# Hybrid SSD and latent-attention layer on one core: twenty softmax scalings from VectorE to GpSimd, with a new order of the instructions

## The chip, the cores and the metric

The kernel runs on one core of one Trainium2 chip. The metric is the device time of one execution in microseconds (us). The engines go by the profile's names: PE is TensorE, PEld its weight loads, DVE is VectorE, ACT is ScalarE, POOL is GpSimd, SP is SyncE.

## The reference, cut to what matters

One layer is computed for two groups of tokens that share the weights: 512 first-chunk tokens, and 64 tokens of a running stream with 256 cached keys. After a norm and an input projection the layer has two branches, a chunked state-space scan (SSD) and latent attention (MLA, 8 heads); both are concatenated, projected, and followed by a SwiGLU feed-forward network of width 2816 and a last norm. What the change touches is the softmax of the attention:

```python
s = (jnp.einsum('bqhl,bkl->bhqk', ql, keys_c, ...)
     + jnp.einsum('bqhr,bkr->bhqk', qr, keys_r, ...))
mask = k_chunk[None, :] <= (qp // CHUNK)[:, None]
s = jnp.where(mask, s * scale, -jnp.inf)
pr = jax.nn.softmax(s, axis=-1).astype(keys_c.dtype)
return jnp.einsum('bhqk,bkl->bqhl', pr, keys_c)
```

Ahead of it the scan's output is gated and normalised, and that result meets the attention's output in `w_out`:

```python
y = y.reshape(b, T, SSD_WIDTH) * jax.nn.silu(z.astype(jnp.float32))
y_ssd = rmsnorm(y, p['ssd_norm']).astype(x.dtype)
...
x = x + jnp.concatenate([y_ssd, o], axis=-1) @ p['w_out']
```

## The kernel before, in words

Activations lie transposed, channels on the 128 partitions and all 576 tokens (512 + 64) along the free axis. Products of full precision are made of three products of rounded halves (`hi` and `lo`, lines 127, 128 and 157, 159): ACT rounds a tile to `hi`, DVE subtracts to get `lo`. Where a weight comes in, ACT casts `wh_...` and DVE makes `wl_...`.

The stages in time: input projection and convolution (to about 87 us), SSD chunks together with the projections `z` and the values `V` (to about 142 us), attention together with the first half of the output projection (to about 214 us), the rest of the output projection, the feed-forward network (to about 590 us), last norm and output.

SSD chunk c (lines 512 to 606): `chunk_a` loads the decay sums `cumb` and makes `xdt` from `ps_x` (L530) and `bt`; `chunk_e` forms on ACT the decays `E` (eight exponentials, L551) and on DVE the end weights `xw` (L500) and the product of `E` with `ps_b` (L560); `chunk_b` multiplies them on PE into `ps_y` (L573), which DVE adds to `xsd` (L578), and adds the carried state through `ps_i` (L584 to 586); `chunk_s` carries the state `h` on (L503, L606). `gate(c)` multiplies `xsd` with the gate `sz` (L629), squares it on ACT (L631) and adds the squares on POOL (L632, L633). A gate tile `sz` is made by `z_tile`: `zh` from `ps_z` (L476), `zt` by a tanh on ACT (L479), their product `sz` on DVE (L480).

After the last gate `norm_y` (line 808) sums over channels on PE (`ps_g`, L810 and L812), forms the factor R on ACT and DVE (`nr_y`, `nr_u`; L186 to L193), spreads it by PE over all partitions (`ps_ry`, L821) and copies it to `Ry` (ACT L825, and POOL L818 for 64 columns). `cat_tile(t)` then scales the four tiles of `xsd` with `Ry` (DVE L828) and splits them into `cat_y` (ACT L157, DVE L159). These are the operands of the first half of the output projection: PE `ps_o` (L465), added to the residual by DVE (L797). Its tiles are PE's reserve of work during attention.

Attention goes by four pairs of heads p. `pair_proj(p)` makes `qs` and `ks` from `ps_q` and `ps_k` (copies L669 and L673), with the rotary rows of `qs` brought by four DMAs from POOL's queue (L663); two buffers of `qs` are used in turn, so that pair 2 waits for the scores of pair 0. `scores(p, i)` has five blocks of queries, i = 0 to 3 with 128 (i + 1) keys for both heads j = 0 and 1, and i = 4, the stream, 128 rows with 320 keys. `soft(p, i)` makes the probabilities `pr` of a block:

```python
for j, s in enumerate(scs):
    dve.tensor_reduce(mx[:, j : j + 1], s, AX, ALU.max, negate=True)
    act.activation(pr[:, j], s, AF.Exp, bias=mx[:, j : j + 1], accum_out=sm[:, j : j + 1])
dve.reciprocal(sm[:, :n], sm[:, :n])
for j in range(n):
    if j:
        act.activation(pr[:, j], pr[:, j], AF.Identity, scale=sm[:, j : j + 1])
    else:
        dve.tensor_scalar(pr[:, j], pr[:, j], sm[:, j : j + 1], None, ALU.mult)
```

These are lines 702 to 709. The last one, L709, runs once a block, 20 times in all. `turn` and `turn_s` transpose the scaled `pr` on PE (`ptp`, L741 and L749) and copy it to `pt`; `values` multiplies it with `V` (`pv`, L766 and L777), and `cat` splits the result (L758, L759).

The order of the work is written out by hand: `issue_in_order` at the end of the kernel chains all instructions of each engine in the order of a table `ISSUE`, one list of numbers an engine, and a second table `PLACES` says which buffer of a pool a tile takes. Each engine runs its list in order and waits where an operand is not there yet. The score tiles `sc` have three PSUM banks in turn, so that a score waits until the exponential of the third score before it has been taken.

Of the kernel before, what the change touches and what calls it, by code (L numbers as in the profile page):

```python
# [11 lines left out]
F32 = mybir.dt.float32  # L12
F32R = mybir.dt.float32r
AF = mybir.ActivationFunctionType
ALU = mybir.AluOpType
# [4 lines left out]
P = 128  # L20
# [36 lines left out]
def hybrid_layer_kernel(ctx: ExitStack, tc: tile.TileContext, a, o):  # L57
    nc = tc.nc
    pe, act, dve, pool, sp = nc.tensor, nc.scalar, nc.vector, nc.gpsimd, nc.sync
# [632 lines left out]
    att_, ap_ = open_pool("att", bufs=1, side="right")  # L692
    prs, pts = {}, {}

    def soft(p, i, scs, nk):

        n = len(scs)
        mx = ap_.tile([P, 2], F32, tag="mx", name="mx", bufs=4)
        sm = ap_.tile([P, 2], F32, tag="sm", name="sm", bufs=4)
        pr = ap_.tile([P, n, nk], F32, tag=f"pr{i}", name=f"pr_{p}_{i}", bufs=2)  # L700
        for j, s in enumerate(scs):
            dve.tensor_reduce(mx[:, j : j + 1], s, AX, ALU.max, negate=True)
# [3 lines that stand above are left out]
            if j:  # L706
                act.activation(pr[:, j], pr[:, j], AF.Identity, scale=sm[:, j : j + 1])
            else:
                dve.tensor_scalar(pr[:, j], pr[:, j], sm[:, j : j + 1], None, ALU.mult)  # L709
        prs[p, i] = pr  # L710
# [689 lines left out]
808-810 792 811-824 835-842 829 849 825-826 850-851 832 830 852 843 833 853 844-845 870 854 846 855-857 847-848  # L1400
858-860 834 871 861-862 872 863 886 873 864-868 887 869 890-892 888 893-895 889 878-885 874-877 896-898 902 911
903-907 912-920 899-901 925 921-924 926-927 908-910 940 949-950 928-931 934 932-933 951-952 935 941-944 953 936-937
954 938-939 955 945-948 956-963 988 964 1000 965 972 989-990 1001-1003 991 973 966 1004-1005 967 992 1006 968 993-994
976-978 995-996 1007-1009 997 979 998-999 969 1010-1011 980 970 981 971 1014-1016 1028-1030 1017 974 982 1018-1019 975
985 1034 983 1035 984 1036-1037 986 1031-1032 987 1038 1033 1039 1044-1049 1012-1013 1020-1027 1066-1071 1060
1072-1074 1061-1062 1040 1050 1075 1042 1051 1076 1041 1077 1063-1064 1043 1052 1065 1053 1078-1089 1054 1106-1107
1090 1108-1112 1056-1057 1055 1113-1117 1058 1130 1059 1091 1131-1132 1100 1118-1125 1133 1092 1126-1127 1134
1128-1129 1135-1137 1104 1101 1138 1096 1214-1217 1097 1139-1140 1098 1218 1141 1099 1219-1221 1105 1093 1222 1143
1094 1223 1142 1102 1226-1227 1224 1228-1231 1095 1225 1103 1232-1235 1144 1236-1237 1161 1145 1250-1251 1162 1146
1252-1254 1238-1241 1164-1165 1255-1257 1242-1243 1173 1166 1244 1167 1258 1245 1163 1168 1259 1246-1249 1155-1160  # L1410
1147-1154 1190-1191 1178 1262 1175-1176 1174 1177 1263 1179 1260 1169 1264 1180 1265-1266 1170 1267 1261 1171 1268
1172 1269 1212-1213 1187 1270 1181 1271 1182 1274 1183 1275 1184 1272 1185 1276 1186 1277 1188 1278 1273 1189
1279-1282 1200-1205 1192-1199 1206-1207 1303 1209 1304 1208 1305 1210 1306 1211 1283 1307 1284-1286 1308 1287-1288
1309 1289-1290 1315 1292 1316 1293 1317 1291 1310 1296 1318 1297 1311 1298-1299 1319 1294-1295 1312 1300 1313 1301
1314 1302 1320 1333-1336 1327-1332 1337-1340 1321-1326 1341-1376 1389-1391 1377-1379 1392-1396 1380 1397-1404
1381-1388 1405-1435 1437 1436 1438-1459 1572 1460 1569 1461-1470 1560 1566 1471-1484 1570 1485-1492 1563-1564 1557
1493-1496 1573 1561 1497-1514 1565 1584 1515 1585 1516-1519 1521 1520 1558 1522-1527 1567 1528 1568 1529 1559 1574
1530-1536 1571 1537-1538 1593 1590-1591 1539-1540 1562 1581 1545-1547 1582-1583 1592 1548-1550 1541-1544 1578
1551-1552 1587 1579-1580 1553-1556 1575-1576 1602 1577 1594 1588 1596 1595 1614 1599 1586 1603 1597 1589 1611 1598
1600-1601 1620 1604 1617 1612 1605-1606 1621-1622 1615 1608-1609 1607 1613 1632 1610 1643 1626-1628 1633 1616  # L1420
1635-1636 1629 1644-1649 1623 1641 1624 1630 1650 1625 1651-1654 1618-1619 1638 1637 1631 1679-1682 1655-1660 1639
1667 1661-1662 1668 1683 1663 1634 1642 1684-1685 1669-1670 1640 1671-1673 1686 1664-1665 1674 1687 1675-1676 1666
1688 1677 1689 1703-1704 1678 1690-1699 1715 1705-1706 1716 1700-1702 1707-1714 1717-1719 1727-1732 1763-1765 1733
1720-1721 1734 1739 1722 1735-1736 1766 1740 1737 1767 1741-1743 1751 1768-1773 1744-1748 1723 1738 1724 1787 1774
1752-1758 1725-1726 1749 1788 1750 1759-1760 1789-1791 1761 1792-1797 1775 1798 1776-1777 1762 1778-1786 1799
1823-1830 1847 1831 1848-1849 1832 1850-1857 1800 1811 1801 1812-1813 1833 1858 1814 1834 1802-1804 1815-1816
1835-1836 1859-1860 1817 1861-1869 1818-1819 1837-1839 1820-1821 1840-1843 1871 1844-1846 1805-1807 1870 1872 1822
1808 1873-1878 1883 1809-1810 1879 1895-1901 1880-1881 1902-1906 1884-1889 1882 1919-1920 1890-1893 1921-1922
1931-1935 1907-1909 1955 1936 1923 1956 1910 1924 1911-1915 2009 1894 1937-1938 1916-1917 1939-1940 2010-2011 1918
2012 1941 2013 1957-1958 2014 1959 1943-1945 1925-1930 1960 1946 1942 2039-2041 1947-1949 2027-2028 1997-1999  # L1430
1985-1986 1950-1953 1961 1954 2029 1987-1988 2000 2042 2001 1962-1964 1989-1990 2043 2030 1973 2031 2033-2034
1974-1975 1965 1991 2003-2004 1966 1992 2005 1976 2002 2032 1967 2006 1993-1994 2035 1977 2044 2036 1978 1968 2007
1995 2037 1996 1979-1981 2038 1982-1983 2008 2045 2051 2046-2047 2052 1969 2021 2063-2065 2048-2049 1984 2053-2055
1970 2050 1971 2015-2017 2066 2056-2058 1972 2069 2059-2061 2070 2022 2018-2019 2062 2067 2071-2073 2023 2020 2075
2068 2099 2074 2100-2101 2076-2081 2102-2107 2024-2026 2082-2083 2087 2108 2088 2177 2089-2092 2084-2086 2093-2098
2111-2113 2123 2109 2124-2126 2114-2119 2127-2128 2120 2129-2133 2121-2122 2134-2136 2178-2181 2165-2166 2110
2141-2146 2167 2182 2153-2154 2137 2155-2156 2147-2150 2138 2195 2151 2207-2208 2196-2199 2157 2200 2159 2168 2201
2158 2139-2140 2213 2160 2152 2161-2162 2214 2202 2169 2163 2215-2216 2170 2209 2164 2217 2210-2212 2218-2219 2171
2183 2172-2175 2220-2221 2184 2176 2185-2186 2237 2222-2230 2203 2187-2189 2238 2204-2205 2239 2190 2206 2255
2191-2192 2256-2260 2267 2240 2243 2241-2242 2193 2268 2231-2232 2244-2246 2233 2269 2261-2264 2194 2247-2248 2234  # L1440
2265 2249 2235-2236 2270-2274 2291 2266 2275-2278 2250-2254 2292-2305 2279-2290 2339 2351-2353 2306-2307 2315-2319
2308-2310 2327 2320-2321 2340-2341 2322-2323 2342 2328-2329 2354 2311 2343 2324 2344 2312 2325 2345-2346 2330-2334
2313 2335-2338 2347 2355-2356 2326 2357 2314 2358 2348 2363-2364 2349-2350 2359-2361 2365-2368 2387 2369 2388-2390
2370-2371 2375-2379 2372-2374 2391 2380-2386 2362 2399-2409 2392-2393 2411-2413 2394-2395 2410 2414 2396 2415 2423
2459 2424 2460 2425-2428 2416 2435-2436 2429 2397 2430 2417-2419 2398 2461 2420-2421 2437-2438 2422 2431 2462-2463
2513-2514 2432 2447-2450 2515 2451 2464 2452-2454 2433-2434 2455-2457 2439-2443 2458 2516-2518 2465-2469 2489 2444
2501 2490 2445 2543 2470-2472 2477 2491 2446 2473 2531 2478-2479 2532-2533 2480 2492 2502 2481 2493-2494 2482 2503
# [238 lines left out]
```

## Time and profile before

| what | value |
| --- | --- |
| median of three runs | 630.3 us (630.15 to 630.4) |
| the profiled execution, its own time | 630.52 us |
| its span, first to last instruction | 628.8 us |
| busy: PE / PEld | 618.6 / 591.4 us |
| busy: DVE / ACT / POOL | 553.9 / 387.0 / 83.1 us |
| mean granted clock of PE | 0.997 |
| HBM read and written | 59.14 MB, 4.15 MB |

The profile is that of one execution. Matmuls are pipelined and their ends are modelled, so a PE that counts as busy may still start fewer matmuls than it could; weight loads overlap with them. In a row of the timeline stand its start, its length, engine, line, operation, the tiles written and read, the shape, and, in brackets, the engine's idle time before it and what ended it. In a row of a group, the busy time, the mean of one in ns, and the idle time follow after the bars. Numbers of instructions stand behind an x.

### The profile page before, as it was taken

To read this page: it belongs to the slowest core of one execution; us is meant where nothing else is said; L and a number is where in the kernel's file an instruction comes from. 1 tells how busy PE (TensorE), PEld (TensorE's weight loads), DVE (VectorE), ACT (ScalarE), POOL (GpSimd) and SP (SyncE) were. 2 spreads that over 40 slices of the span, in tenths; PEclk is the share of its full clock that TensorE was granted. 3 is DMA by queue.
4 is the path that set the end of the run, shared out by engine and by line. 5 is a ranking of instruction groups with operands and counts; after the bars stand their busy time and mean duration, and the time that the engine had idled before them with its cause. 6 is when DMAs were issued, how large, how long until landed. Compare 5 with 4: busy or idle time off the path is not lost.

```text
span 628.8 us, 11891 instructions
## 1 busy us (share of the span) xinstructions
PE 618.6 (98%) x4591; PEld 591.4 (94%) x4591; DVE 553.9 (88%) x979; ACT 387.0 (62%) x744; POOL 83.1 (13%) x123
## 2 busy tenths in 40 slices
PE   9999999999999999999999999999999999999995
PEld 9899999976887899999999999999999999999994
DVE  6899996999876799999999997799888998999766
ACT  7555336689767489766556565555665656645454
POOL 1332241232100000000112001100210011100023
PEclk9999999999999999999999999999999999999998
DMA  9512195332311222322467137460764274725005
GB/s 314 211 36 95 36 222 153 101 101 104 118 68 34 102 101 78 112 82 68 117 161 191 54 120 186 105 167 11 200 173 114 68 185 112 188 70 185 22 1 185
DMA packets 32889, 74.64 MB, mean 119 GB/s; under 512 B 3882, under 2 KB 11960, under 8 KB 32576
## 3 DMA queue, kind: packets, MB, share of 16 engines
q1 hardware_dynamic: 26688, 62.73, 30.7%
q0 software_dynamic: 5424, 10.57, 9.4%
q8 instruction: 36, 0.59, 0.4%
q10 hardware_dynamic: 720, 0.57, 0.3%
q14 instruction: 21, 0.17, 0.1%
HBM read 59.14 MB, written 4.15 MB: 101 GB/s over the span
## 4 chain that ended last, share of the span: by engine, by line
PE 95%; DVE 2%; ACT 1%; issue 0%; DVEq 0%; POOL 0%; ACTq 0%; POOLq 0%
PE ps_x L947 21%; PE ps_z L947 11%; PE ps_dx L1087 9%; PE ps_o L465 8%; PE ps_in L143 8%; PE ps_y L947 5%; PE ps_dz L1087 5%; PE ps_z L465 4%; PE ps_l L1157 3%; PE ps_first L143 3%; PE ps_dy L1087 2%; PE ps_p L947 2%; PE sc L719 2%; PE pv L766 1%; PE ptp L741 1%; PE ps_q L465 1%
## 5 line engine op out<-in xcount | busy, mean ns | idle before, releaser
L947 PE MATMUL ps_x<-xop,wh_gu_S 128*128 128x288 f32 x504 | 120.8, 296 | 0.0
L947 PEld LDWEIGHTS ps_x<-xop,wh_gu_S 128*128 128x128 f32 x504 | 86.1, 188 | 0.6 <-ACT u L1016 0.3
L947 PE MATMUL ps_x<-xop,wl_gu_S 128*128 128x288 f32 x252 | 73.9, 295 | 0.0
L947 PE MATMUL ps_z<-xop,gu_a 128*128 128x288 f32 x252 | 57.5, 295 | 0.0
L127 ACT CAST wh_gu_S<-gu 128x1024 fp32r<-128x1024 f32 x44 | 46.0, 1052 | 15.8 <-PE ps_y L947 7.0
L128 DVE TENSOR_TENSOR wl_gu_S<-gu,wh_gu_S 128x1024 fp32r<-128x1024 f32 x44 | 53.4, 1223 | 1.5 <-ACT wh_gu_S L127 1.2
L1100 POOL DMA_DIRECT2D x<-db x16 | 14.6, 945 | 279.2 <-ACT db L1093 243.8
L947 PEld LDWEIGHTS ps_x<-xop,wl_gu_S 128*128 128x128 f32 x252 | 47.2, 188 | 0.0
L143 PE MATMUL ps_in<-xs,wh_in 128*128 128x288 f32 x256 | 45.4, 297 | 0.0
L947 PE MATMUL ps_z<-xop,wh_gu_S 128*128 128x288 f32 x168 | 42.6, 295 | 0.0
L947 PE MATMUL ps_y<-xop,wh_gu_A 128*128 128x288 f32 x168 | 42.2, 295 | 0.0
L947 PEld LDWEIGHTS ps_z<-xop,gu_a 128*128 128x128 f32 x252 | 41.9, 188 | 0.0
L947 PE MATMUL ps_x<-xop,wh_gu_A 128*128 128x288 f32 x168 | 40.1, 295 | 0.0
L143 PEld LDWEIGHTS ps_in<-xs,wh_in 128*128 128x128 f32 x256 | 37.7, 188 | 0.7 <-ACT wh_in L127 0.5
L127 ACT CAST wh_gu_A<-gu 128x1024 fp32r<-128x1024 f32 x22 | 23.1, 1050 | 15.4 <-PE ps_x L947 11.2
L465 PE MATMUL ps_o<-cat_y,wh_out 128*128 128x288 f32 x128 | 31.9, 329 | 0.1
L128 DVE TENSOR_TENSOR wl_gu_A<-gu,wh_gu_A 128x1024 fp32r<-128x1024 f32 x22 | 26.9, 1224 | 3.6 <-ACT wh_gu_A L127 2.5
L947 PEld LDWEIGHTS ps_y<-xop,wh_gu_A 128*128 128x128 f32 x168 | 29.3, 188 | 0.1
L947 PEld LDWEIGHTS ps_z<-xop,wh_gu_S 128*128 128x128 f32 x168 | 29.4, 188 | 0.0
L947 PEld LDWEIGHTS ps_x<-xop,wh_gu_A 128*128 128x128 f32 x168 | 28.6, 188 | 0.0
L143 PE MATMUL ps_in<-xs,wl_in 128*128 128x288 f32 x128 | 27.8, 295 | 0.0
L465 PE MATMUL ps_z<-xs,wh_z 128*128 128x288 f32 x128 | 27.5, 306 | 0.0
(611 smaller groups left out, 2017.8 us busy)
## 6 DMA issues: line engine op xcount, KB each, us to landing
gu<-in_w_gu SPq DMA_DIRECT2D x44, 512.0 KB, 4.6
db<-in_w_down SPq DMA_DIRECT2D x16, 512.0 KB, 4.6
x<-db POOLq DMA_DIRECT2D x16, 288.0 KB, 5.5
x<-dc POOLq DMA_DIRECT2D x16, 288.0 KB, 4.2
wr_in<-in_w_in SPq DMA_DIRECT2D x8, 512.0 KB, 5.0
wr_out<-in_w_out SPq DMA_DIRECT2D x8, 512.0 KB, 3.3
cumb<-cumD SPq DMA_DIRECT2D x5, 512.0 KB, 5.6
x<-in_xT SPq DMA_DIRECT2D x2, 1152.0 KB, 5.8
```

The costliest lines, as they stand in the source:

```text
L127: act.copy(hi, raw)
L128: dve.tensor_tensor(lo, raw, hi.bitcast(F32), ALU.subtract)
L143: pe.matmul(ps[:m, hf, :n], w, x[:, hf * n : (hf + 1) * n], start=start and k == 0 and i == 0, stop=stop and k == last and i == 2,)
L465: pe.matmul(ps[:, :n], w, x[:, cols], start=not onto and k == 0 and i == 0, stop=onto or (k == len(terms) - 1 and i == 2), skip_group_chec ...
L719: pe.matmul(s[:, :nk], qs[:, j, q0 : q0 + P], ks[:, j, :nk], start=True, stop=True)
L741: pe.transpose(pp[:, k : k + P], prs[p, i][:, j, b * P : b * P + P], ident)
L766: pe.matmul(pv[64 * j : 64 * j + 64, b * P :], V[b][:, h * HD : (h + 1) * HD], pts[p, b, j], start=b == 0, stop=True, skip_group_check=b > 0,)
L947: pe.matmul(ps, p, q, start=not onto and first and kp == kps[0] and j == 0, stop=onto or (last and kp == kps[-1] and j == 2), skip_group_c ...
L1087: pe.matmul(ps, l, r, start=not onto and k == 0 and j == 0, stop=onto or (k == n - 1 and j == 2), skip_group_check=onto,)
L1100: pool.dma_start(x2[t], v, accum_op=ALU.add)
L1157: pe.matmul(ps, w, x[:, cols], start=first and not onto and k == 0 and i == 0, stop=onto or (last and k == len(terms) - 1 and i == 2), ski ...
```

## The change

Three edits. L709 is issued on POOL and not on DVE. The small tiles `mx` and `sm` (two columns) have 20 buffers and not 4. The `ISSUE` lists of PE, DVE and ACT are ordered anew between the end of the SSD chunks and the beginning of the feed-forward network, and POOL's list has 20 entries more. SP's list and the table `PLACES` stay as they are.

```diff
@@ -695,8 +695,8 @@
         n = len(scs)
-        mx = ap_.tile([P, 2], F32, tag="mx", name="mx", bufs=4)
-        sm = ap_.tile([P, 2], F32, tag="sm", name="sm", bufs=4)
+        mx = ap_.tile([P, 2], F32, tag="mx", name="mx", bufs=20)
+        sm = ap_.tile([P, 2], F32, tag="sm", name="sm", bufs=20)
...
             else:
-                dve.tensor_scalar(pr[:, j], pr[:, j], sm[:, j : j + 1], None, ALU.mult)
+                pool.tensor_scalar(pr[:, j], pr[:, j], sm[:, j : j + 1], None, ALU.mult)
...
     "POOL": """
...
-58-59 70-71 68-69 72-85 87 86 88-89 91 90 92-97 99 98 100-101 103 102 104-105 107 106 108-118 120-121 119 123 122
+58-59 70-71 68-69 73 72 74-75 82-84 76 85 77-80 88-91 81 87 86 93 92 94-96 99 98 97 100-105 107 106 108-109 111 110
+112-117 119 118 120-121 123 122 124-125 127 126 128-138 140-141 139 143 142
```

Three places show what the lists do. The first is DVE's list near the end of the SSD chunks (minus: before, plus: changed); `zh_1516` is the last gate tile's projection, `sz<-zt_1398` the tile before it, `wl_pair` the weights of pair 1.

```order
 L500 TENSOR_TENSOR xw_1506<-xdt_1484,E_1496 128x512
 L560 TENSOR_TENSOR E_1496<-E_1496,ps_b_1486 128x512
+L480 SCALAR_TENSOR_TENSOR sz<-zt_1398,zh_1397 128x576
 L476 SCALAR_TENSOR_TENSOR zh_1516<-ps_z_0_1518,R_99 128x288
 L560 TENSOR_TENSOR E_1496<-E_1496,ps_b_1486 128x512
 L476 SCALAR_TENSOR_TENSOR zh_1516<-ps_z_1_1544,R_99 128x288
-L480 SCALAR_TENSOR_TENSOR sz<-zt_1398,zh_1397 128x576
+L128 TENSOR_TENSOR wl_pair_1816<-wr_pair_1813,wh_pair_1815 128x384
```

The older `sz` has moved ahead of the first half of `zh_1516`, and the weights of pair 1 have moved up.

The second place is PE's list at `ps_y` of chunk 3 (`ps_y_1836`); `ps_q` and `ps_k` here are projections of pair 0, `ps_s` and `ps_i` the states.

```order
+L507 MATMUL ps_s_1830<-xw_1707,bt_1615 128x256
+L465 MATMUL ps_k_1_1798<-ckv,wh_pair_1754 128x416 x2
+L465 MATMUL ps_q_1_1804<-cqn_487,wh_pair_1754 128x288
 L465 MATMUL ps_q_1_1804<-cqn_487,wl_pair_1755 128x288
-L507 MATMUL ps_s_1830<-xw_1707,bt_1615 128x256
+L465 MATMUL ps_k_1_1798<-ckv,wl_pair_1755 128x416
 L573 MATMUL ps_y_1836<-E_1734,xdt_1722 64x128 x8
-L465 MATMUL ps_k_1_1798<-ckv,wh_pair_1754 128x416 x2
-L465 MATMUL ps_k_1_1798<-ckv,wl_pair_1755 128x416
```

The second half of pair 0's `k` projection has moved from behind `ps_y` of chunk 3 to ahead of it.

The third place is the beginning of attention, on two engines. On DVE, from the scaling of pair 0's block 2 to the first `cat_y`:

```order
-L709 TENSOR_SCALAR pr_2_1967<-pr_2_1967,sm 128x384
+L828 SCALAR_TENSOR_TENSOR xsd<-xsd,par,Ry 128x576
+L702 TENSOR_REDUCE mx<-sc_s 128x1
 L828 SCALAR_TENSOR_TENSOR xsd<-xsd,par,Ry 128x576
 L704 RECIPROCAL sm<-sm 128x2
-L702 TENSOR_REDUCE mx<-sc_s 128x1
-L709 TENSOR_SCALAR pr_0_1981<-pr_0_1981,sm 128x128
-L828 SCALAR_TENSOR_TENSOR xsd<-xsd,par,Ry 128x576
 L702 TENSOR_REDUCE mx<-sc_3_0_1999 128x1
 L159 TENSOR_TENSOR cat_y_1936<-xsd,cat_y_1936 128x576
```

Two scalings are gone from between the `Ry` products, and the rest stands in nearly the same order. On POOL, at the same time (`qs_382` is the buffer of pairs 0 and 2):

```order
 L633 TENSOR_TENSOR R_99<-ysq_1860 128x128
+L709 TENSOR_SCALAR pr_3_1927<-pr_3_1927,sm 128x512
 L818 COPY Ry<-R_99 128x64
-L663 DMA qs_382<-rrp 16x576 x4
+L709 TENSOR_SCALAR pr_1_1953<-pr_1_1953,sm 128x256
+L709 TENSOR_SCALAR pr_2_1967<-pr_2_1967,sm 128x384
+L663 DMA qs_382<-rrp 16x576 x3
+L709 TENSOR_SCALAR pr_0_1981<-pr_0_1981,sm 128x128
+L663 DMA qs_382<-rrp 16x576
+L709 TENSOR_SCALAR pr_4_1994<-pr_4_1994,sm 128x320
```

The five scalings of pair 0 stand around the copy to `Ry` and the four DMAs that bring the rotary rows of pair 2.

More of the change, by code (lines that the diff above doesn't have):

```diff
@@ new lines @@
+819 811 810 821 825 827 835 812 836 854 829 828 830-831 839 837-838 844 841 858 845 840 855 850 847 856 851-853 846
+849 863 848 859 864 862 876 857 870 861 880 882 871-872 860 877 873 879 884 881 865 883 874 887 842 878 885 892 894
+866 895 886 896 893 867 843 888 868 891 897 890 889 898-901 910 875 904 911 905 902 906 869 903 912 907 914 908 913
+909 919 917 923 918 916 920 915 922 921 924-925 927 926 928-929 931 936 933 932 930 934-935 939 937 942 938 946 943
+940 947 941 944 949 945 950-951 948 952-958
```

322 lines of the change are left out of this document (158 added, 164 removed).

## The prediction

> **What bounds the kernel now.** I read the page first, then a table of busy time by stage, then TensorE's own waits in the stage that is left.
>
> ```profile
> span 628.8 us, 11891 instructions
> ...
> PE 618.6 (98%) x4591; PEld 591.4 (94%) x4591; DVE 553.9 (88%) x979; ACT 387.0 (62%) x744; POOL 83.1 (13%) x123
> ...
> PE 95%; DVE 2%; ACT 1%; issue 0%; DVEq 0%; POOL 0%; ACTq 0%; POOLq 0%
> ```
>
> The chain that ended last is 95% PE, so a faster VectorE is worth only what PE waits for it. The table by stage (columns: stretch, length, then busy us and instructions of PE, PEld, DVE, ACT, POOL, the granted clock, DMA) says where that is:
>
> ```profile
> 115.00:155.00 40.00, 38.69 (x264) 30.33 (x263) 38.61 (x83) 34.32 (x86) 10.95 (x17) 1.00 0.36 113
> 155.00:215.00 60.00, 60.00 (x451) 48.93 (x450) 42.76 (x106) 39.93 (x106) 1.92 (x4) 1.00 0.18 63
> 215.00:560.00 345.00, 344.96 (x2591) 343.87 (x2590) 321.20 (x518) 214.61 (x373) 27.71 (x32) 1.00 0.45 122
> ```
>
> Between 115 and 155 us VectorE is busy 38.6 of 40 us and PE falls short; from 155 to 215, where most of the twenty scalings stand, VectorE has 17 us to spare and PE none. So the change can only pay in the 40 us in which the last SSD chunks end and attention begins. There PE and its weight loads wait as follows (in brackets: idle time before the row, and what ended it):
>
> ```profile
> 135.72 0.95 PEld L573 LDWEIGHTS ps_y<-E,xdt 128*64 128x64 f32 x16 [0.91 <-ACT qs L669]
> 139.77 0.30 PEld L810 LDWEIGHTS ps_g<-R,ones 128*128 128x128 f32 x2 [0.40 <-issue]
> 141.96 0.30 PEld L465 LDWEIGHTS ps_q<-cqn,wh_pair 128*128 128x128 f32 x2 [0.81 <-ACT ks L673]
> 143.79 0.30 PEld L719 LDWEIGHTS sc<-ks,qs 100*128 100x128 f32 x2 [0.62 <-ACT pr L703]
> 147.48 0.97 PEld L821 LDWEIGHTS ps_ry<-R,ident 128*128 128x128 f32 x8 [0.42 <-DVE R L193]
> 149.68 0.30 PEld L719 LDWEIGHTS sc<-ks,qs 100*128 100x128 f32 x2 [0.68 <-ACT pr L703]
> 151.25 0.50 PEld L741 LDWEIGHTS ptp<-ident,pr 128*128 128x128 f32 x3 [0.42 <-DVE pr L709]
> 153.25 0.19 PEld L465 LDWEIGHTS ps_o<-cat_y,wh_out 128*128 128x128 f32 x1 [0.73 <-DVE cat_y L159]
> ```
>
> ```profile
> 135.75 1.16 PE L573 MATMUL ps_y<-E,xdt 128*64 128x128 f32 x16 [0.54 <-ACT ks L673]
> ...
> 143.80 0.70 PE L719 MATMUL sc<-ks,qs 100*128 100x256 f32 x2 [0.21 <-ACT pr L703]
> ...
> 147.49 1.16 PE L821 MATMUL ps_ry<-R,ident 128*128 128x128 f32 x8 [0.23 <-DVE R L193]
> ```
>
> The eight idle times of the weight loads add up to 5.0 us; part of that is covered by matmuls still running. PE's own three add up to 1.0 us; those leave out short gaps. The truth lies between, and I take the middle, 3 us, as all that can be won. The last of these waits is for VectorE's `cat_y`; behind it PE has dense work.
>
> **The change part by part.** The twenty scalings cost VectorE this:
>
> ```profile
> L709 DVE TENSOR_SCALAR pr<-pr,sm x20: 277/382/486, 145.4 to 204.6; 128x512 f32<-128x512 f32 x4, 128x256 f32<-128x256 f32 x4, 128x384 f32<-128x384 f32 x4, 128x128 f32<-128x128 f32 x4
> ```
>
> 20 x 0.38 = 7.6 us, but only those ahead of the first `cat_y` lie on the path. These are the rows of VectorE and ScalarE that make it:
>
> ```profile
> 112.84 0.67 ACT L479 ACTIVATE zt<-zh 128x576 f32<-128x576 f32 x1
> ```
> ```profile
> 117.89 0.46 DVE L476 SCALAR_TENSOR_TENSOR zh<-ps_z,R 128x288 f32<-128x288 f32 x1 [0.66 <-PE ps_z L465]
> ...
> 145.37 0.47 DVE L709 TENSOR_SCALAR pr<-pr,sm 128x512 f32<-128x512 f32 x1
> ...
> 146.61 0.35 DVE L192 TENSOR_TENSOR nr_u<-nr_u,nr_v 128x192 f32<-128x192 f32 x1
> ...
> 149.24 0.41 DVE L709 TENSOR_SCALAR pr<-pr,sm 128x384 f32<-128x384 f32 x1
> 149.73 0.82 DVE L828 SCALAR_TENSOR_TENSOR xsd<-xsd,par,Ry 128x576 f32<-128x576 f32 x1
> ...
> 150.92 0.28 DVE L709 TENSOR_SCALAR pr<-pr,sm 128x128 f32<-128x128 f32 x1
> 151.11 0.81 DVE L828 SCALAR_TENSOR_TENSOR xsd<-xsd,par,Ry 128x576 f32<-128x576 f32 x1
> ...
> 152.44 0.75 DVE L159 TENSOR_TENSOR cat_y<-xsd,cat_y 128x576 fp32r<-128x576 f32 x1
> ```
> ```profile
> 145.90 0.36 ACT L189 ACTIVATE nr_u<-nr_y 128x192 f32<-128x192 f32 x1
> ...
> 148.68 0.58 ACT L825 COPY Ry<-ps_ry 128x512 f32<-128x512 f32 x1
> ```
>
> Four terms, in order of time:
>
> 1. *The new order alone.* At 117.89 VectorE had waited 0.66 us for PE. The new order puts the gated tile `sz` (L480) there, whose `zt` was ready at 112.84 + 0.67 = 113.5. VectorE is full from there to the last SSD gate, so all behind comes 0.66 us earlier. ScalarE's exponentials of chunk 2 and 3 are moved up too and should keep pace; it is busy 34.3 of these 40 us.
> 2. *nr_u.* Its input from ScalarE is there at 145.90 + 0.36 = 146.26, it starts at 146.61: the queue ahead of it held the first scaling (0.47 us). That is gone: 0.35 us.
> 3. *The first L828.* `Ry` is there at 149.26, L828 starts at 149.73 behind the scaling of 149.24: 0.47 us.
> 4. *The second L828.* The scaling at 150.92 takes 0.19 us until L828 starts at 151.11.
>
> Sum 1.67 us, by which the first `cat_y` comes earlier. PE's reordering (a `k` projection ahead of `ps_y` of chunk 3) covers the 0.91 us wait at 135.72, but by itself only moves it: PE would meet the same chain later. It is counted at nothing; what it costs if the cover fails is that 0.91 us again. PE's later reorderings, the ScalarE order and four more changes of matmul kind are nothing as well, since the same work stands in a stage in which PE is never idle. The 20 instead of 4 buffers of `mx` and `sm` are two columns each; no row waits for them, nothing.
>
> What POOL's scaling costs is not in the trace. Nearest rows of POOL, one input, then two:
>
> ```profile
> L545 POOL TENSOR_SCALAR_AFFINE_SELECT cumb<-cumb 128x1024 f32<-128x1024 f32 x4 | 4.4, 1110 | 15.4 <-ACT el L520 15.4
> ...
> L632 POOL TENSOR_TENSOR ysq<-ysq 128x256 f32<-128x256 f32 x4 | 2.9, 732 | 12.4 <-ACT ysq L631 12.4
> ...
> L1248 POOL TENSOR_TENSOR ss<-ss,sq 128x320 f32<-128x320 f32 x3 | 2.6, 871 | 60.5 <-ACT sq L1243 60.4
> ...
> L818 POOL COPY Ry<-R 128x64 f32<-128x64 f32 x1 | 0.2, 236 | 3.0 <-DVE R L193 3.0
> ```
>
> With one input 64 columns take 236 ns and 1024 take 1110: (1110 - 236) / 960 = 0.91 ns a column, so 512, 384, 320, 256 and 128 columns take 0.64, 0.53, 0.47, 0.41 and 0.29 us, 2.34 us a pair of heads. With two inputs it is (871 - 732) / 64 = 2.17 ns a column, 1.29, 1.01, 0.87, 0.73 and 0.45 us, 4.35 us a pair. A scaling has one input of that size, so I take the first and keep the second for the range. POOL has 58 us of idle time between 155 and 215, so its total is covered.
>
> In POOL's queue stand DMAs too:
>
> ```profile
> 149.85 2.02 POOL L663 DMA_DIRECT2D qs<-rrp  x4 [2.12 <-PE sc_s L725]
> ```
>
> They wait for PE's last score of pair 0, about 0.5 us each. Three of them are now ahead of the scaling of `pr_0_0`, which the first transposes need: it would start at 149.85 + 1.5 = 151.35, less the 0.7 to 1 us by which the scores come earlier, and VectorE did it at 150.92. Nothing, give or take 0.3. Their own landing moves by up to 1.5 us; `qs` of pair 2 is read some 15 us later.
>
> Last, a price for running both engines at once. The same VectorE instruction with two SBUF inputs, `xw`, first alone, then while POOL reads SBUF:
>
> ```profile
> 115.74 0.69 DVE L500 TENSOR_TENSOR xw<-xdt,E 128x512 f32<-128x512 f32 x1
> ...
> 127.16 1.39 DVE L500 TENSOR_TENSOR xw<-xdt,E 128x512 f32<-128x512 f32 x1
> ```
> ```profile
> 126.93 1.08 POOL L545 TENSOR_SCALAR_AFFINE_SELECT cumb<-cumb 128x1024 f32<-128x1024 f32 x1
> ```
>
> It took 0.70 us longer and ended 0.5 us behind POOL's. L828, `nr_u`, R and `cat_y` have two SBUF inputs as well, and five scalings fall between 146 and 153 us. Bounds: the most is a whole scaling ahead of both L828 and `cat_y` (0.53 + 0.29 + 0.47 = 1.29 us lost); on the other side, the earlier `xw` may now miss the POOL instruction that cost it 0.70 us (a gain). I take a loss of 0.3, nearer the middle of the two, since it is chance which starts first.
> The Trainium skill, "SBUF — State Buffer", section "Who interferes with whom", speaks against the change here: "A DVE instruction with two SBUF inputs contends with a GpSimd instruction that reads SBUF", and the second to start is blocked until the first ends. The 1.39 us row agrees. Taken at its hardest this rule leaves 1.67 - 1.29 = 0.4 us; by the middle of the rows it is 1.4.
>
> Sum: 1.67 - 0.3 = 1.4 us. The profiled execution took 630.52 us, its span 628.8 and 1.7 around it: 630.5 - 1.4 = 629.1. The median of the three runs, 630.3, is 0.2 below the profiled one: **628.9**.
>
> **The rivals.**
>
> *Given back at the port.* POOL's scalings hold up L828 and `cat_y` as above, at 1.29 us. For it: the 1.39 us row, and five scalings within 7 us. Against: VectorE's other work there (row maxima, copies) reads PSUM, and often POOL will be the one to wait. Gain 0.4: 630.3 - 0.4 = 629.9.
>
> *Slower: POOL delivers late.* Pair 3's five scalings stand together at the end of POOL's queue, and pair 3's transposes follow the values of pair 2 with only the last output tiles between them. At the price of two inputs POOL needs 4.35 us for a pair, and if a third of the scalings meets a VectorE instruction that holds them for the 0.70 us of `xw`, 5 x 0.23 = 1.15 us more: 5.5 us for what cost VectorE 5 x 0.38 = 1.9. That is 3.6 us late, which PE would wait out, since no later pair is left. 3.6 less the 1.4 won is 2.2 slower: 632.5. A scaling of (1.9 + 1.4) / 5 = 0.66 us on average, waits included, eats the gain; over 0.92 us it is slower by more than 0.2%. Against: one input only, and between the transposes of pair 3 stand output tiles that need no scaling.
>
> *All waits go.* The order searched anew removes all 3 us of PE's waits: 630.3 - 3.0 = 627.3. For it: PE now has projections in front of `ps_y`. Against: the waits for `Ry` and `cat_y` follow from a chain through five engines that the change shortens only by the four terms.
>
> **How the numbers follow.** About 0.2%, 1.3 us, is what a measurement of this kernel can tell from no change: below 629.0 is faster, above 631.6 slower by more than it. Forecast 0.48, own range a gain of 0.9 to 2.1 (628.2 to 629.4); given back 0.26; slower 0.14; all waits 0.12. Of the forecast about 0.65 lies below 629.0: faster 0.48 x 0.65 + 0.12 = 0.43; same 0.17 + 0.26 = 0.43; slower 0.14. Range 627.6 to 631.0: it reaches down to where half of the case of all waits lies and up past the given-back case, with its unknown of 0.7 us on the port, and leaves out about 2 in 10, most of it in the slower case.
>
> **What would show it.** Right: the row at 117.89 has lost its 0.66 us; `cat_y` starts between 150.5 and 151.5; L709 shows 20 rows on POOL with a mean of 0.4 to 0.6 us; PE's first `ps_o` comes 1 to 2 us earlier and PE stays dense to 215. Given back: L828 or L159 of over 1.2 us. Slower: waits of PE for POOL `pr` on L741, above all between 200 and 212. Wrong altogether: a VectorE that idles between 118 and 142 for PE or ScalarE, so that term 1 is lost.

## The result, and the profile after

| | before | after |
| --- | --- | --- |
| median | 630.35 us (630.15 to 630.44, 4 runs) | 638.81 us (638.34 to 639.8, 4 runs) |
| span of the profiled execution | 628.8 us | 636.6 us |
| mean granted clock of PE | 0.997 | 0.994 |

The ratio is 1.0137, 95% interval 1.0119 to 1.0154: 8.5 us slower, far above the predicted range. Executions far out of the rest, one each of experiments 1, 5 and 7 and of the kernel before (1224.81, 3445.21, 861.94 and 1297.44 us), are left out of every ratio below. First the engines' busy times on the page of the changed kernel, then its table by stage, with the same columns as that of before.

```profile
PE 620.2 (97%) x4591; PEld 591.2 (93%) x4591; DVE 547.2 (86%) x959; ACT 386.2 (61%) x744; POOL 107.7 (17%) x143
```
```profile
115.00:155.00 40.00, 37.30 (x256) 29.06 (x256) 37.16 (x78) 32.63 (x83) 17.17 (x22) 1.00 0.36 113
155.00:215.00 60.00, 55.57 (x390) 44.36 (x388) 34.30 (x82) 38.20 (x104) 20.38 (x20) 0.97 0.17 58
```

VectorE lost 6.7 us of work (the prediction had 7.6), and GpSimd gained 24.6. But from 155 to 215 us, where PE was busy all 60 us before, it now starts 390 matmuls instead of 451. The waits from 115 to 225 us name the reason (waiting engine and line, whom it waits for, us in total, times, longest):

```profile
PE ptp L741 <- POOL pr L709: 6.8, 4, 2.3
```

PE waits four times, once a pair of heads, for a scaling on GpSimd. In the timeline of PE each has its row (in brackets the idle time before it):

```profile
153.58 0.33 PE L741 MATMUL ptp<-ident,pr 128*128 128x128 f32 x1 [2.33 <-POOL pr L709]
...
170.13 0.33 PE L741 MATMUL ptp<-ident,pr 128*128 128x128 f32 x1 [1.42 <-POOL pr L709]
...
196.73 0.33 PE L741 MATMUL ptp<-ident,pr 128*128 128x128 f32 x1 [2.30 <-POOL pr L709]
...
213.73 0.33 PE L741 MATMUL ptp<-ident,pr 128*128 128x128 f32 x1 [0.71 <-POOL pr L709]
```

What a scaling costs there, over all five shapes (busy us, then the mean of one in ns):

```profile
L709 POOL TENSOR_SCALAR pr<-pr,sm 128x512 f32<-128x512 f32 (+4 forms) x20 | 24.8, 1250 | 36.7 <-DVE sm L704 33.6
```

Twenty at 1.25 us make 25.0 us, where the prediction had 0.47 on average, 0.87 at the price of two inputs and 1.10 with waits at the port. GpSimd's timeline shows how they stand:

```profile
150.29 1.53 POOL L663 DMA_DIRECT2D qs<-rrp  x3
151.86 1.67 POOL L709 TENSOR_SCALAR pr<-pr,sm 128x128 f32<-128x128 f32 x1
...
190.80 5.88 POOL L709 TENSOR_SCALAR pr<-pr,sm 128x512 f32<-128x512 f32 x5 [11.35 <-DVE sm L704]
```

The five scalings of pair 2 run in one row of 5.88 us, after GpSimd has waited 11.35 us for a reciprocal. Yet four of the five reciprocals were there before that one; VectorE's timeline has them at

```profile
184.22 0.17 DVE L704 RECIPROCAL sm<-sm 128x2 f32<-128x2 f32 x1 [1.63 <-ACT pr L703]
...
187.18 0.15 DVE L704 RECIPROCAL sm<-sm 128x1 f32<-128x1 f32 x1
...
188.08 0.15 DVE L704 RECIPROCAL sm<-sm 128x2 f32<-128x2 f32 x1
...
189.15 0.17 DVE L704 RECIPROCAL sm<-sm 128x2 f32<-128x2 f32 x1 [0.92 <-ACT pr L703]
...
190.48 0.16 DVE L704 RECIPROCAL sm<-sm 128x2 f32<-128x2 f32 x1
```

VectorE's new list takes the reciprocals of pair 2 in the order of blocks 2, 4, 1, 0, 3. GpSimd's list asks for them in the order 3, 2, 4, 1, 0. So the scaling whose operand comes last stands at the head of the queue, the other four stand behind it, and block 0, which PE needs first, comes last of all, at 190.80 + 5.88 = 196.68. PE's row of 196.73 follows at once.

One thing more is lost. PE's table by single microseconds (the number after the bracket is the granted clock):

```profile
155.00:156.00 1.00, 1.00 (x5) 0.52 0.02 2
156.00:157.00 1.00, 1.00 (x6) 0.50 0.00 0
157.00:158.00 1.00, 1.00 (x6) 0.50 0.00 0
158.00:159.00 1.00, 1.00 (x9) 0.78 0.00 0
```

Shortly behind the first wait PE ran at half clock for some 3.4 us: 0.48 + 0.50 + 0.50 + 0.22 = 1.7 us lost. The four waits of 6.8 us and this make 8.5 us; the span is 7.8 us longer, so that some 0.7 us was won elsewhere (0.27 of it ahead of the change, as the part on the prediction shows). The loss at half clock differs between executions: the mean granted clock was 0.994 in two of the four and 0.992 in the two longest (639.01 and 639.8 us).

### The profile page after: what moved, and what is told of

Read it like the earlier page. It is cut to its first block, busy times and chain, and to the rows that moved or that the text cites. A ratio compares the mean times of both kernels' runs of the same rounds, so it can differ in the third digit from the quotient of the medians.

```text
span 636.6 us, 11915 instructions
## 1 busy us (share of the span) xinstructions
PE 620.2 (97%) x4591; PEld 591.2 (93%) x4591; DVE 547.2 (86%) x959; ACT 386.2 (61%) x744; POOL 107.7 (17%) x143
## 4 chain that ended last, share of the span: by engine, by line
PE 63%; DVE 1%; DMA 1%; ACT 1%; issue 0%; POOL 0%; DVEq 0%; ACTq 0%
PE ps_x L947 21%; PE ps_z L947 10%; PE ps_dx L1087 9%; PE ps_y L947 5%; PE ps_o L465 5%; PE ps_dz L1087 4%; PE ps_l L1157 3%; PE ps_dy L1087 2%; PE ps_p L947 2%; DMA x<-db 1%; PE pv L766 0%; PE ptp L741 0%; ACT sq L1243 0%; DVE x L1200 0%; POOL pr L709 0%
## 5 line engine op out<-in xcount | busy, mean ns | idle before, releaser
L465 PE MATMUL ps_o<-cat_y,wh_out 128*128 128x288 f32 x128 | 33.2, 340 | 0.0
L709 POOL TENSOR_SCALAR pr<-pr,sm 128x512 f32<-128x512 f32 (+4 forms) x20 | 24.8, 1250 | 36.7 <-DVE sm L704 33.6
```

What stands on the lines that cost most here:

```text
L465: pe.matmul(ps[:, :n], w, x[:, cols], start=not onto and k == 0 and i == 0, stop=onto or (k == len(terms) - 1 and i == 2), skip_group_chec ...
L709: pool.tensor_scalar(pr[:, j], pr[:, j], sm[:, j : j + 1], None, ALU.mult)
```

## The experiments

Ratios are against the kernel before on the same chip, with their 95% intervals.

**1. The new order, scalings on VectorE.** The new lists of PE, ACT and DVE; each scaling is put back on VectorE, one instruction behind its reciprocal.

```diff
-                pool.tensor_scalar(pr[:, j], pr[:, j], sm[:, j : j + 1], None, ALU.mult)
+                eng = dve if True else pool
+                z = eng.tensor_scalar(pr[:, j], pr[:, j], sm[:, j : j + 1], None, ALU.mult)
...
```

> The changed kernel with its new lists for PE and ACT, but the twenty scalings back on VectorE, each one instruction behind its reciprocal. Theory (a scaling on POOL takes 0.6 to 1.57 us, 0.27 us and 2.5 ns a column, and PE waits for it): the waits of PE for POOL, 6.8 us in the changed kernel, are gone, and of the terms of the prediction the 0.66 us of the new order stays: 628.5 to 630.5 us. Rival one (the new lists themselves are the loss): 636 us or more. Rival two (the shared port holds VectorE up): as the theory.

Measured 631.87 us, ratio 1.0018 (1.0009 to 1.0028). This lies above the 630.5 of my theory and far below the 636 of the first rival: the waits for GpSimd are the bulk of the loss, and the new order, with the scalings in these places on VectorE, is no gain but a loss of 1.1 us.

**2. The old order, scalings on GpSimd.** The lists of before without the scalings on VectorE, GpSimd's list of the changed kernel, and its 20 buffers.

> The lists of PE, ACT and VectorE of before, with the twenty scalings on POOL in the changed kernel's POOL list. Theory: the old lists ask for the scaled tiles no later than the new ones, so PE waits as long or longer: 637 to 643 us. Rival one (the new lists are the loss): 630 to 632 us.

Measured in a single execution: 631.61 us, within the spread of the kernel before on that chip (629.73 to 631.65). My expectation of 637 to 643 fell: the same instruction on the same engine at the same price costs about 1 us here. GpSimd's timeline shows why:

```profile
151.62 0.61 POOL L709 TENSOR_SCALAR pr<-pr,sm 128x128 f32<-128x128 f32 x1
...
176.88 1.56 POOL L709 TENSOR_SCALAR pr<-pr,sm 128x512 f32<-128x512 f32 x1 [2.27 <-DVE sm L704]
184.99 1.25 POOL L709 TENSOR_SCALAR pr<-pr,sm 128x384 f32<-128x384 f32 x1 [6.55 <-DVE sm L704]
187.59 2.56 POOL L709 TENSOR_SCALAR pr<-pr,sm 128x320 f32<-128x320 f32 x3 [1.35 <-DVE sm L704]
```

In the old order block 3 of pair 2 has its reciprocal first and not last. The five scalings come as their operands come, spread over 13 us, and the last ends at 190.15, in time for PE. PE has one wait for a scaling left, the first, behind the DMAs:

```profile
152.29 0.55 PE L741 MATMUL ptp<-ident,pr 128*128 128x128 f32 x3 [0.93 <-POOL pr L709]
```

So neither the price nor the new order makes the loss by itself.

**3. The price taken away.** GpSimd scales only the first 32 columns of each tile; the other columns stay unscaled.

```diff
-                pool.tensor_scalar(pr[:, j], pr[:, j], sm[:, j : j + 1], None, ALU.mult)
+                pool.tensor_scalar(pr[:, j, :32], pr[:, j, :32], sm[:, j : j + 1], None, ALU.mult)
```

> The changed kernel, but each scaling on POOL treats only the first 32 columns of its tile, the others stay unscaled; waits, queues and lists are the same. Theory (the price a column): a scaling takes 0.27 + 32 x 0.0025 = 0.35 us, and the time falls to what was predicted, 628.5 to 630 us. Rival one (lists): 636 us or more. Rival three (the fixed cost, the hand-over between engines or the DMAs in POOL's queue make the tiles late): 633 us or more.

Measured 630.62 us, ratio 1.0001 (0.9992 to 1.0010), a little above the 628.5 to 630 of the theory and well below both rivals: all of the loss is gone with the columns, though PE still waits 1.27 us for the first scaling.

**4. PE's wait taken away.** GpSimd scales as in the changed kernel, except that of 512 columns it takes only 384 and that its scalings follow each other in the program's order; it writes the result aside, and PE takes the unscaled tiles.

```diff
-                pool.tensor_scalar(pr[:, j], pr[:, j], sm[:, j : j + 1], None, ALU.mult)
+                m = min(nk, 384)
+                z = pool.tensor_scalar(R1[:, 192 : 192 + m], pr[:, j, :m], sm[:, j : j + 1], None, ALU.mult)
...
```

> The changed kernel, but POOL writes the scaled tile aside, into free columns of R1 (of 512 columns only 384), so that PE transposes the unscaled tile and waits for ScalarE alone; POOL works as long as before and still shares the port. Its scalings follow each other in the program's order. Theory (PE's wait for a late tile is the loss): 629 to 631 us. Rival two (the port: POOL blocks VectorE): 633 us or more, with L828, L159 and L128 well longer than before.

Measured 629.81 us, ratio 0.9991 (0.9982 to 1.0000). GpSimd's work beside VectorE's gives no loss against the kernel before; PE's waiting for its results does. It may still eat into the gain; the part on the prediction comes back to that.

**5. GpSimd's queue sorted.** One line of GpSimd's list: the scalings of a pair stand in the order of their reciprocals, and that of pair 0, block 0 stands ahead of three DMAs.

```diff
-58-59 70-71 68-69 73 72 74-75 82-84 76 85 77-80 88-91 81 87 86 93 92 94-96 99 98 97 100-105 ...
+58-59 70-71 68-69 73 72 74-75 76 82-85 77-78 80 79 88-91 81 87 93 92 94-95 86 97 96 98 100 99 101-105 ...
```

> The changed kernel with its twenty scalings on GpSimd and the new lists of TensorE, VectorE and ScalarE as they are; only GpSimd's list is sorted: within each pair the scalings stand in the order in which VectorE's new list takes their reciprocals, and the scaling of pair 0, block 0 stands ahead of three DMAs. Theory 'wrong place in the queue': in the changed kernel four tiles of pair 2 lie ready from 184.4 to 189.3 us, but the queue asks for block 3 first, whose reciprocal comes at 190.63; then all five stand in a row, 5.9 us. Sorted, only one scaling (1.6 us) is left behind the last reciprocal, and the first transposes need others: of the 8 us at least 6.5 come back, 630.0 to 632.0 us, PE waits for L709 under 1 us. Rival 'the price alone' (25 us of GpSimd time, whatever the order): 634 to 638 us.

Measured 632.5 us, ratio 1.0030 (1.0019 to 1.0042), just above the range expected: four fifths of the loss come back by the order of one queue. Its rows are from a further execution:

> The sorted kernel again, unchanged, for an undisturbed profile. By the theory PE waits for L709 only at short notice: at the stream block of pair 0, and at block 1 of pair 1, some 3 us together, nothing over 0.5 us in pairs 2 and 3, and its clock stays at 1.00, since no idle time of 2.5 us is left. Time 632 to 633 us.

631.99 us; PE's timeline has two waits for GpSimd left, both at short notice, as expected; 3 us of waits were expected and 2.2 came:

```profile
155.31 0.33 PE L749 MATMUL ptp_s<-ident,pr 128*128 128x128 f32 x1 [1.69 <-POOL pr L709]
...
168.18 0.33 PE L741 MATMUL ptp<-ident,pr 128*128 128x128 f32 x1 [0.49 <-POOL pr L709]
```

**6. The same, but the first scaling stays behind the DMAs.** Sorted in pairs 1 to 3 alone.

> As the sorted kernel, but only pairs 1, 2 and 3 are sorted; the scaling of pair 0, block 0 stays behind the three DMAs. Theory: the first wait of PE (2.5 us) stays, and with it the stretch at half clock behind it; together 2.5 to 3.5 us, so 633 to 635 us, and PE's clock is near 0.5 again just behind the wait. If the clock is chance, it is 632 to 633 with a clock of 1.00. Rival 'the price alone': 634 to 638.

Measured 634.48 us, ratio 1.0057 (1.0042 to 1.0073). Against experiment 5 the first wait costs 2 us. The half clock comes back with it in the profiled execution, of 635.56 us, in PE's table:

```profile
153.00:154.00 1.00, 0.00 (x0) 0.96 0.14 32
154.00:155.00 1.00, 0.84 (x4) 0.50 0.00 0
155.00:156.00 1.00, 1.00 (x6) 0.50 0.21 53
```

But it does not come back each time. Two of the four executions took 633.28 and 633.68 us at a mean clock of 0.996, the other two 635.29 and 635.56 us at 0.994 and 0.993. As far as the mean clocks tell, the wait alone costs about 1 us, and the half clock, where it comes, some 2 us more.

**7. The old order, first scaling ahead of the DMAs.** As experiment 2, with `76 82-85` in place of `82-84 76 85` in GpSimd's list.

> The lists of before with the scalings on GpSimd, and the scaling of pair 0, block 0 ahead of the four DMAs instead of behind three of them. In the run with it behind them, that scaling started 1.5 us behind its reciprocal and the first transpose came 0.8 us later than before; this is the whole difference up to 400 us. Theory: that 0.8 us comes back, 629.8 to 630.8 us: old lists carry the dear scaling for nothing, and gain nothing. Rival 'contention at the SBUF port': it stays at 631 to 632.

Measured 630.16 us, ratio 0.9994 (0.9985 to 1.0003). The old lists carry the dear scaling for nothing.

**8 and 9. The most urgent scalings on VectorE.** The sorted kernel with one, then with three scalings put back.

> The sorted kernel, with the one scaling that the first transpose waits for (pair 0, block 0, 128 columns) on VectorE, behind its reciprocal and two row maxima; the other nineteen on GpSimd. Theory: the early terms (about 1.3 us at the first output tile) are kept, since this scaling costs VectorE 0.28 us and is not late: 629.0 to 630.3 us, at or a little below the kernel before. Rival 'the new order gives nothing back behind attention' : 630.3 to 631.5, like the new order with all scalings on VectorE.

> The sorted kernel with the three scalings on VectorE that the new TensorE list asks for soonest (pair 0 block 0, pair 0 stream block, pair 1 block 1); the other seventeen on GpSimd. In the run with one on VectorE, PE still waited 1.7 us for the stream block, which stood behind four DMAs in GpSimd's queue, and 1.3 us for pair 1 block 1. Theory 'short notice': these two waits were what kept that run 1.5 us behind; without them 629.4 to 630.6 us. Rival 'the new order itself costs 1 us wherever the scalings run': 631 to 632, like the new order with all scalings on VectorE.

With one: 632.16 us, ratio 1.0029 (1.0017 to 1.0040), a miss. Both waits of experiment 5 stayed, 1.69 us for the stream block, which stands behind the four DMAs, and 0.49 us. With three: 630.44 us, ratio 0.9991 (0.9982 to 1.0000), as expected; no wait of PE for a scaling on GpSimd is left. Two waits of 2.2 us together (3.2 us by the weight loads) stood between those two kernels; their ratios differ by 0.0038, 2.4 us.

**10. What the instruction costs.** A price list, on the sorted kernel.

> A price list, on the sorted kernel. Pair 0 as it was (per-row scale from sm), pair 1 scaled by a constant, pair 2 multiplied by sm spread along the row as a second operand, pair 3 only copied onto itself; pairs 1 and 3 are thus not scaled by their sums. Theory A, the operation tensor_scalar is dear: pair 1 costs the same 2.5 ns a column as pair 0, pair 2 about 2.2 (as the kernel's other two-input rows), pair 3 about 0.9. Theory B, the per-row operand is dear: pair 1 falls to about 0.9 ns a column.

The rows by shape, the widest and the narrowest of each form (L710 per-row scale, L712 scaled by a constant, L714 second operand, L716 copy):

```profile
L710 POOL TENSOR_SCALAR pr<-pr,sm 128x512 f32<-128x512 f32 x1 | 1.6, 1571 | 3.1 <-DVE sm L704 3.1
L712 POOL TENSOR_SCALAR pr<-pr 128x512 f32<-128x512 f32 x1 | 1.5, 1549 | 0.0
...
L714 POOL TENSOR_TENSOR pr<-pr,sm 128x512 f32<-128x512 f32 x1 | 1.0, 1041 | 0.6 <-DVE sm L704 0.6
...
L716 POOL COPY pr<-pr 128x512 f32<-128x512 f32 x1 | 0.6, 608 | 0.0
L710 POOL TENSOR_SCALAR pr<-pr,sm 128x128 f32<-128x128 f32 x1 | 0.6, 604 | 0.3 <-DVE sm L704 0.3
L712 POOL TENSOR_SCALAR pr<-pr 128x128 f32<-128x128 f32 x1 | 0.5, 538 | 0.0
...
L714 POOL TENSOR_TENSOR pr<-pr,sm 128x128 f32<-128x128 f32 x1 | 0.4, 399 | 0.6 <-DVE sm L704 0.6
L716 POOL COPY pr<-pr 128x128 f32<-128x128 f32 x1 | 0.3, 296 | 2.7 <-ACT pr L703 2.7
```

The one execution took 632.17 us. Differences over 384 columns: 2.52 ns a column scaled per row, 2.63 by a constant, 1.67 with a second operand, 0.81 for a copy. It is the operation that is dear, not the per-row operand (theory A); the same product with two inputs is a third cheaper, and cheaper than the 2.2 that theory A had for it.

**11. The cheaper form in the changed kernel.** All four lists as in the changed kernel, one edit:

```diff
-                pool.tensor_scalar(pr[:, j], pr[:, j], sm[:, j : j + 1], None, ALU.mult)
+                pool.tensor_tensor(pr[:, j], pr[:, j], sm[:, j : j + 1].to_broadcast([P, nk]), ALU.mult)
```

> The changed kernel with one edit: GpSimd multiplies by sm as a second operand spread along the row, instead of scaling by a per-row operand; 512 columns 1.04 us instead of 1.57, 384 0.83, 320 0.72, 256 0.61, 128 0.40. All four lists as in the changed kernel. By the theory (late requests in a row) the row of five in pair 2 takes 3.6 us instead of 5.9, so that wait of PE is gone or under 0.3 us; pair 1 waits 0.2 instead of 1.6 us, pair 3 nothing; the first wait stays near 2 us since the three DMAs stand ahead. 633.0 to 635.0 us. Rival 'the order of GpSimd's list is the whole loss': 637 to 639. Rival 'the price is the whole loss': 630 to 631.5.

Measured 630.53 us, ratio 0.9997 (0.9988 to 1.0006). My expectation of 633 to 635 was wrong and the rival's held: at this price the unsorted queue costs nothing that can be measured. The group of its scalings, their row of five in GpSimd's timeline, PE's one wait (pair 0), and its weight loads in pairs 1 and 2:

```profile
L709 POOL TENSOR_TENSOR pr<-pr,sm 128x512 f32<-128x512 f32 (+4 forms) x20 | 16.2, 829 | 36.6 <-DVE sm L704 32.7 <-ACT wh_pair L127 3.5 <-issue 0.4
```
```profile
186.12 3.43 POOL L709 TENSOR_TENSOR pr<-pr,sm 128x512 f32<-128x512 f32 x5 [11.90 <-DVE sm L704]
```
```profile
152.02 0.33 PE L741 MATMUL ptp<-ident,pr 128*128 128x128 f32 x1 [0.82 <-POOL pr L709]
```
```profile
165.47 0.14 PEld L741 LDWEIGHTS ptp<-ident,pr 128*128 128x128 f32 x1 [0.20 <-POOL pr L709]
...
189.61 0.14 PEld L741 LDWEIGHTS ptp<-ident,pr 128*128 128x128 f32 x1 [0.44 <-POOL pr L709]
```

The row of five ends at 186.12 + 3.43 = 189.55, and the weight load of 189.61, which has waited 0.44 us for it, follows at once. Nothing is to spare there: in pairs 1 and 2 the matmuls still running cover these short waits, so the new lists bear this price and hardly more. The wait of 0.82 us in pair 0 is left, and the time is that of the kernel before all the same.

**12 to 14. Is there a gain to be had?** Two-input products in the kernel with three scalings on VectorE, in the old order, and in the sorted kernel with all twenty on GpSimd.

> The kernel with three scalings on VectorE and seventeen on a sorted GpSimd list, those seventeen as two-input products. PE had no wait for L709 on GpSimd left there, so theory: no change by the cheaper form, 629.6 to 630.6 us, a gain of about 0.5 us over the kernel before. Rival 'less contention at the SBUF port': another 0.5 us, 629.0 to 629.6.

> The lists of before, all twenty scalings on GpSimd as two-input products, the first one ahead of the DMAs. Theory: the old lists left VectorE a reserve nearly everywhere; what is won is the time of the scalings ahead of the first output tiles, 0.3 to 0.8 us: 629.5 to 630.3 us. Rival: no change at all, 630.3 to 630.7.

> The sorted GpSimd list (the scaling of pair 0, block 0 ahead of three DMAs) and two-input products, all twenty on GpSimd. Against the run with two-input products in the unsorted list, only the first wait of PE changes (0.8 us). Theory 'the first wait takes the gain': 629.5 to 630.2 us, faster than before by 0.5 to 1. Rival 'the gain ends elsewhere, the stream block behind the four DMAs now waits instead': 630.3 to 631.2.

Measured 631.06 us (1.0004, 0.9995 to 1.0013), 630.29 us (0.9995, 0.9986 to 1.0003) and 629.90 us (0.9991, 0.9982 to 1.0000). The first missed both of its expectations, and why it is no faster than the kernel of experiment 9 is open. The second lies where its theory (to 630.3) and its rival (from 630.3) meet, and decides nothing; the third came out as its theory said. The best of all versions is about 0.5 us ahead of the kernel before, at the edge of what can be told and below the 0.2% of the prediction.

## Why the prediction was wrong

**The four terms came true in their sum, not one by one.** Rows of VectorE, then of ScalarE, in the changed kernel:

```profile
115.47 0.69 DVE L500 TENSOR_TENSOR xw<-xdt,E 128x512 f32<-128x512 f32 x1
...
116.88 0.75 DVE L480 SCALAR_TENSOR_TENSOR sz<-zt,zh 128x576 f32<-128x576 f32 x1
117.62 0.46 DVE L476 SCALAR_TENSOR_TENSOR zh<-ps_z,R 128x288 f32<-128x288 f32 x1
...
145.23 0.36 DVE L192 TENSOR_TENSOR nr_u<-nr_u,nr_v 128x192 f32<-128x192 f32 x1
...
148.21 1.02 DVE L828 SCALAR_TENSOR_TENSOR xsd<-xsd,par,Ry 128x576 f32<-128x576 f32 x1
...
149.55 0.80 DVE L828 SCALAR_TENSOR_TENSOR xsd<-xsd,par,Ry 128x576 f32<-128x576 f32 x1
150.28 0.15 DVE L704 RECIPROCAL sm<-sm 128x2 f32<-128x2 f32 x1
...
150.94 0.74 DVE L159 TENSOR_TENSOR cat_y<-xsd,cat_y 128x576 fp32r<-128x576 f32 x1
```
```profile
144.78 0.36 ACT L189 ACTIVATE nr_u<-nr_y 128x192 f32<-128x192 f32 x1
...
147.31 0.59 ACT L825 COPY Ry<-ps_ry 128x512 f32<-128x512 f32 x1
```

`xw` stands ahead of the first instruction that the new lists move, and it already starts 0.27 us earlier than the 115.74 of before. So 0.27 us has to come off every comparison of the two traces. The gate tile `sz` stands at 116.88, and `zh` behind it no longer waits; ScalarE's `nr_u` starts 1.12 - 0.27 = 0.85 us earlier, where term 1 had 0.66. Of term 2's 0.35 us 0.26 came, since `nr_u` on VectorE now starts 0.09 us behind its input. Of term 3's 0.47 only 0.16: `Ry` is there at 147.90, and the first L828 still starts 0.31 us later. The contention took 0.2 us from it (1.02 instead of about 0.8), near the 0.3 set down. `cat_y` starts 1.50 us earlier, within the 150.5 to 151.5 named, but that is 1.23 with the 0.27 off, against a forecast of 1.4. That the sum came so near is in part luck: term 1 made up for term 3.

**The step that failed: "A scaling has one input of that size, so I take the first".** The price was taken from other one-input operations, 0.91 ns a column, and held between that and two inputs, 2.17. It is 2.52, above both. An AFFINE_SELECT and a COPY say nothing of a TENSOR_SCALAR, and the number of inputs does not order the prices: two inputs cost 1.67. The five scalings of a pair were set down at 2.34 us; by the rows of the changed kernel they cost 25.0 / 4 = 6.25, above the 5.5 of the worst case.

**"POOL has 58 us of idle time ..., so its total is covered" failed beside it.** The total is covered, the due times are not. What counts is for how long each block's scaling may run between its reciprocal and its transpose, in the queue order, and for that the new lists leave little. PE's later reorderings and the rest of the new order were set down as nothing, "since the same work stands in a stage in which PE is never idle". They were not nothing: in the old order the same scalings cost about 1 us or nothing (experiments 2 and 7), in the new one 8.5. For the forecast I followed GpSimd's queue in pair 0 alone. There the three DMAs were to cost nothing "give or take 0.3"; they and the scaling of 1.67 us behind them cost 2.33 us.

**The rival "slower: POOL delivers late" had the mechanism, but neither the size nor the place.** It put 3.6 us of lateness on pair 3, 2.2 with the gain taken off. The lateness came at all four pairs: 2.33, 1.42, 2.30 and 0.71 us, and pair 3's was the least. Its point of decision, a mean of 0.66 us to eat the gain and 0.92 to be slower by over 0.2%, fits what was measured: 1.25 us is slower, 0.83 (experiment 11) is neither. What spoke against it in the prediction, "one input only", was the mistaken price.

**Why the 1.4 us do not appear even without the waits.** The sum followed `cat_y`, but PE's list asks for the transposes of `pr_0_0` ahead of the first output tile, and their reciprocal did not come earlier by 1.4. Before it stood at

```profile
150.46 0.16 DVE L704 RECIPROCAL sm<-sm 128x2 f32<-128x2 f32 x1
```

and after at 150.28, which with the 0.27 us off is 0.1 us later and not earlier. The new list of VectorE has two L828 ahead of it, where there was one. But this reciprocal is not the whole limit: in experiment 4 PE's transposes need neither it nor a scaling, and the gain was only 0.73 us (629.81 against 630.54), little more than the 0.56 of experiment 14 (629.90 against 630.46). Rows of VectorE and PE in experiment 4 (where L830 is the L828 of the changed kernel), then of VectorE in experiment 14:

```profile
152.56 1.38 DVE L830 SCALAR_TENSOR_TENSOR xsd<-xsd,par,Ry 128x576 f32<-128x576 f32 x1
```
```profile
154.67 0.40 PE L465 MATMUL ps_o<-cat_y,wh_out 128*128 128x288 f32 x1 [0.40 <-DVE cat_y L159]
```
```profile
152.95 1.44 DVE L828 SCALAR_TENSOR_TENSOR xsd<-xsd,par,Ry 128x576 f32<-128x576 f32 x1
```

The last L828 takes 1.38 and 1.44 us, where it took 0.82 before, and in experiment 4 PE waits for the `cat_y` behind it. But in experiments 9 and 12, where the scaling beside it is on VectorE, it took 0.80 and 0.81 us, and no more was gained. So how much of the missing gain this is stays open.

**The rival "given back at the port"** was real. Its sign, an L828 of over 1.2 us, does not show in the changed kernel (1.08 at most) but does in those two and in experiment 11 (1.27). The Trainium skill, "SBUF — State Buffer", section "Who interferes with whom", names the pair that meets here, a VectorE instruction with two SBUF inputs and a GpSimd instruction that reads SBUF, and says that the order of issue decides which of them is blocked. The trace agrees that GpSimd can be the one: the 128-column scaling at 151.86, started behind the L828 of 151.61 and with a `cat_y` beside it, took 1.67 us; the one of 0.60 us in experiment 10 shows its price where nothing holds it up. So some 1.1 of the 2.33 us of PE's first wait came from there. The two L828 above do not fit the rule by their start times: GpSimd's scalings beside them start at 152.79 and 153.02, behind them, and yet it was L828 that took longer. The prediction had said against this rival that POOL would often be the one to wait; because PE waited for GpSimd, this was no comfort.

What is shown: the loss needs both the price of the form (experiments 3 and 11 take it away, with the order as it is) and the order of the queues (experiments 2, 5 and 7 take away most or all of it, with the price as it is). What stays open: where between 116 and 240 us the new order with the scalings on VectorE loses its 1.1 us (its trace is 0.49 us ahead of that of before at 116 us and 0.70 behind at 240), and why the half clock follows the first wait and not the third, which is as long. For the second the traces offer a reading that no run tested. The half clock lasted 3.413 us in both traces that have it, and the full clock ahead of it 150.19 and 146.77 us, 44 and 43 times as long, as if the clock were set in steps of that length. In the changed kernel the step before the half clock then held 1.96 us without a matmul, in experiment 6 some 2.1; the third wait was cut by the end of a step into 1.56 and 0.74. That two of the four executions of experiment 6 kept the full clock would fit, since the same wait can fall otherwise upon the steps. Idle time alone would not be the whole rule: at the end of experiment 14's kernel a step with 1.3 us of it was followed by half clock, while in experiment 10 one with 1.69 us was not.

## What to carry to other kernels

Price a moved instruction by its own operation on the new engine: where no row shows it, a different operation of the same size is no bound, and a list of measured prices is cheaper than an argument. An engine with spare time is no cover by itself; hold each result's notice, from its operand to its reader, against the price of all that stands ahead of it in the queue. In a queue in order, put first what is ready first: one scaling at the head that waits makes the four behind it late. Before two traces are compared by their times, compare a row ahead of the first change, and take the difference off.

## What was not expected of the hardware

On GpSimd a TENSOR_SCALAR on fp32 took 2.52 to 2.63 ns a column, whether its scalar came from a tile or was a constant; the two-input TENSOR_TENSOR took 1.67 and a COPY 0.81 (experiment 10). PE's granted clock fell to 0.50 for 3.4 us behind the idle time of 2.33 us that ended at 153.58, in the changed kernel, and for 3.4 us at the same place of experiment 6, there in two of four executions by their mean clocks; behind the 2.30 us that ended at 196.73 it did not, nor behind the 1.69 us of experiment 5.
